# Gates of the recurrent mixer as a seven-product block product, with summed factors kept in DRAM and an output projection over all heads

## The chip, the cores and the metric

One core of a Trainium2 chip runs the whole program. The core has five engines with their own instruction streams: TensorE (PE, matmuls; PEld are its weight loads), VectorE (DVE), ScalarE (ACT), GpSimd (POOL) and SyncE (SP, here only an issuer of DMAs). The metric is the device time of one execution in microseconds; less is better. Times are medians of several runs.

## The reference, cut to what matters

A two-layer encoder over 512 + 256 tokens of width 1024. Each layer is a half-weighted feed-forward, a mixer, and another half-weighted feed-forward, each with its RMS norm and residual. Layer 0's mixer is a bidirectional gated linear recurrence with eight heads of 128, layer 1's is windowed attention. The change is in the recurrent mixer:

```python
def hgrn2_mixer(x, w_in, w_o, g_norm, lb):
    q, i, g, f_fw, f_bw = jnp.split(x @ w_in, 5, axis=-1)
    ...
    o_fwd = gla_chunk_scan(q, k_f, i, logf_f)
    o_bwd = rev(gla_chunk_scan(rev(q), rev(k_b), rev(i), rev(logf_b)))
    o = (o_fwd + o_bwd).astype(F32)
    o = o * lax.rsqrt(jnp.mean(o * o, axis=-1, keepdims=True) + NORM_EPS)
    o = o * g_norm.astype(F32).reshape(H, V)
    o = o.reshape(B, T, H * V).astype(x.dtype) * jax.nn.silu(g)
    return o @ w_o
```

`g` is the gate: 768 tokens by 1024 columns of x times a 1024 by 1024 piece of `w_in`.

## The kernel before, in words

The 768 tokens are 6 blocks of 128, in two halves of three blocks. Float32 matmuls are made of three: each operand is split into a high and a low part, and high x high, high x low and low x high are summed in one PSUM bank (`mm3`, L307 to L311). The lower part of a weight is a VectorE subtraction after a ScalarE cast (L172 and L173 for a piece of 128x1024; L314 and L315 for pieces that lie in other buffers).

The recurrent mixer (`hgrn`) goes through these stages. Chunks of head 0 are projected. The value projection is a block product of 2x2 blocks by seven products instead of eight (`tok_quad`): the token operands are four plain blocks or sums of them (b00, b10, b11 and the sums t1 to t4, named in `FACTOR`), the weight operands are sums of weight blocks made on VectorE (L255), and the products are combined by adds from PSUM. Its matmuls have line L729. Then come eight scans, one a head (`hgrn_scan`). A scan has seven levels; at each, VectorE multiplies packed keys and queries by decay factors (L848, L852), ScalarE copies the packed part (L826), TensorE makes the scores (L796), and VectorE copies them under a mask (L815). After the levels, keys are turned (L868), block states are made (L876, L887) and outputs (L900). `weave` puts a fixed number of pieces of other matmuls between the steps of a scan: the projection chunks of the next heads, and beside head 7 the first half of the gates.

The gates are two plain projections of 512 columns (`proj_tok`, "g0" and "g1"): eight k-tiles of three matmuls for each block. ScalarE takes the Silu from PSUM (L995), VectorE multiplies value, inverse RMS and gate, 128 columns at a time (L1001), TensorE turns the result (L1019), and ScalarE and VectorE write its high and low parts (L1022, L1023). The output projection (`out_proj`) goes twice through both column halves, for heads 0 to 3 and 4 to 7, and adds each to x in a separate addition (L570). x itself lies in DRAM during the mixer and is reloaded by ScalarE's queue.

A scheduler decides the order of the instructions on each engine from the order in which the code issues them and from when buffers come free. What bounds it: 21 arena slots of 6144 bytes a partition ("big"), 8 weight slots of 4096 bytes ("w"), 4 raw weight buffers ("wr"), 8 temporaries ("tA") and 8 PSUM banks ("ps"). Weight loads go out on SP in the order planned by `plan_hgrn`, as far ahead as raw buffers allow; every engine's queue is served in order.

Of the kernel before, what the change touches and what calls it, by code (L numbers as in the profile page):

```python
# [50 lines left out]
class Trunk:  # L51
# [73 lines left out]
    def load_masks(self):  # L125
        raw, self.masks = self.big([P, LEVELS + 1, P]), self.big([P, LEVELS + 1, P], U8)
        self.nc.scalar.dma_start(raw, self.consts[1])
        self.nc.gpsimd.tensor_copy(self.masks, raw)
# [280 lines left out]
    def operand(self, name, k):  # L409
        t = self.ops[(name, k // 2)]  # L410
        return t[:, k % 2, 0, :], t[:, k % 2, 1, :]
# [301 lines left out]
    def tok_quad(self, key, tile):  # L713
        nc = self.nc
        cols = lambda b, c: tile(b)[:, c * 512 : (c + 1) * 512]
        banks = {}
        for name in TOK:
            ws = [self.take((*key, name, kp)) for kp in range(2)]
            chain = {"p2": "p1", "p4": "p5", "p3": "p7"}.get(name, name)
            for i in range(HB):  # L720
# [16 lines left out]
                x11, x12, x21, x22 = cols(i, 0), cols(HB + i, 0), cols(i, 1), cols(HB + i, 1)  # L737
                if name == "p1":
                    nc.scalar.activation(x22, ps, AF.Copy, scale=-1.0)
                elif name == "p2":  # L740
                    nc.scalar.copy(x11, ps)
                elif name == "p4":
                    nc.vector.tensor_add(x21, ps, x22)
                elif name == "p3":
                    nc.vector.tensor_sub(x12, ps, x22)
                elif name == "p5":
                    nc.vector.tensor_sub(x22, x22, ps)
                else:
                    nc.vector.tensor_add(x22, ps, x22)
            for kp in range(2):  # L750
                self.done((*key, name, kp))
            yield name
# [45 lines left out]
    def hgrn_scan(self, hd, v):  # L798
# [63 lines left out]
        kT = self.big([P, 8, P])  # L862
        S = self.big([P, 8, P])
# [37 lines left out]
        for s, (off, n) in enumerate(SEQS):  # L901
            nb = n // P
            sq = self.tmp(n)
            nc.scalar.square(sq, pos[s])
            for b in range(nb):
                nc.scalar.copy(vb(off // P + b), pos[s][:, b * P : (b + 1) * P])
            nc.vector.tensor_reduce(
                self.hss[:, h, off // P : off // P + nb], sq.rearrange("p (b j) -> p b j", b=nb), AX.X, ALU.add
            )

    def plan_hgrn(self, w_in, w_o):
# [6 lines left out]
        rows = w_in[:, D : 2 * D].rearrange("(k m a p) c -> k m p a c", k=2, m=2, p=P)  # L918
        srcs = [[rows[k][m][:, :, c * 512 : (c + 1) * 512] for m in range(2)] for c in range(2) for k in range(2)]
        self.plan_quad(("v",), srcs, None, TOK)  # L920
# [4 lines left out]
        self.plan_tok("g0", w_in, 2 * D)  # L925
        self.plan_tok("g1", w_in, 2 * D + 512)
        self.plan_out("hg_o", w_o)

    def plan_out(self, tag, w_o):
        for half in range(2):  # L930
            for c in range(2):
# [9 lines left out]
    def hgrn(self, lb_row, gn_row, next_row):  # L941
# [19 lines left out]
        for name in self.tok_quad(("v",), vtile):  # L961
            if name == "p6":
# [11 lines left out]
        feed = stream()  # L974
        lead = 4
# [12 lines left out]
        uT = {}  # L988

        def put_g(half):  # L990
            us = {}

            def f(s, b, ps):
                sg = self.tmp(512)
                nc.scalar.activation(sg, ps, AF.Silu)  # L995
                off, n = SEQS[s]
                nb = n // P
                u = self.tmp(512)
                for i in range(4):
                    h = half * 4 + i  # L1000
                    nc.vector.scalar_tensor_tensor(  # L1001
                        u[:, i * P : (i + 1) * P],
                        vs[off // P + b][:, h * P : (h + 1) * P],
                        rs[:, h, off // P + b : off // P + b + 1],
                        sg[:, i * P : (i + 1) * P],
                        ALU.mult,
                        ALU.mult,
                    )
                us[(s, b)] = u
                if b < nb - 1:  # L1010
                    return
                def rest():
                    for i in range(4):
                        h = half * 4 + i
                        if s == 0:
                            uT[h] = self.big([P, 2, T], F32R)
                        pt = self.ps(n)
                        for bb in range(nb):
                            nc.tensor.transpose(pt[:, bb * P : (bb + 1) * P], us[(s, bb)][:, i * P : (i + 1) * P], self.ident)  # L1019
# [409 lines left out]
```

## Time and profile before

| what | value |
|---|---|
| median of 3 runs | 2788.37 us (2788.32 to 2788.64) |
| profiled execution | 2788.47 us |
| its span, first to last instruction | 2786.7 us |
| TensorE busy | 2762.9 us, 99% |
| weight loads of TensorE | 2569.4 us, 92% |
| VectorE busy | 2191.5 us, 79% |
| ScalarE busy | 1343.8 us, 48% |
| GpSimd busy | 376.8 us, 14% |
| granted TensorE clock | 0.999 |
| DMA, mean over the span | 106 GB/s |

Of the span, the recurrent mixer takes about 490 to 1035 us: the value projection 542 to 599, the scans 599 to 935, the second half of the gates and the output projection after that. A group's row in the profile gives line, engine, operation, output <- input with shapes and count, then busy time in us and mean length in ns, then the time that the engine was idle just before, and who ended it. In the chain of waits a row is start, length, engine, line and count; a row of stretches gives the busy time and count of each engine in order, the granted clock, the DMA share and the rate.

### The profile page before, as it was taken

How to read it: one execution, taken by the hardware profiler on the slowest of the kernel's cores; microseconds unless marked ns; L12 is line 12 of the kernel's file. 1: busy time of each engine (PE TensorE's matmuls, PEld its weight loads, DVE VectorE, ACT ScalarE, POOL GpSimd, SP SyncE). 2: the span in 40 equal slices, each digit the busy share in tenths (PEclk: the TensorE clock that was granted, in tenths of full speed). 3: DMA queues.
4: the chain of work that ended last, by engine and by line, in shares of the span. 5: the costliest groups of instructions: out<-in, count | busy, mean ns of one | idle time of the engine just before them, and what ended most of it. 6: DMA issues, size and time to landing. Idle time of an engine off the chain costs nothing.

```text
span 2786.7 us, 40646 instructions
## 1 busy us (share of the span) xinstructions
PE 2762.9 (99%) x15189; PEld 2569.4 (92%) x15189; DVE 2191.5 (79%) x3803; ACT 1343.8 (48%) x2479; POOL 376.8 (14%) x409
## 2 busy tenths in 40 slices
PE   8999999999999999999999999999999999999998
PEld 8999999989999889999999999999988889999998
DVE  8788788777887658878878887887848878778877
ACT  7344444634444435444444643444458855444443
POOL 2111111100000001211111121111002311211110
PEclk9999999999999999999999999999999999999999
DMA  6554554421111223555444365545422122655543
GB/s 176 125 131 114 123 144 128 145 69 39 39 39 31 81 81 81 144 134 124 121 114 121 84 144 127 131 114 122 129 72 76 40 66 74 148 133 129 117 114 107
DMA packets 331750, 294.53 MB, mean 106 GB/s; under 512 B 11848, under 2 KB 258080, under 8 KB 331552
## 3 DMA queue, kind: packets, MB, share of 16 engines
q1 hardware_dynamic: 294560, 213.42, 25.7%
q0 software_dynamic: 32688, 65.03, 13.9%
q10 hardware_dynamic: 4304, 13.49, 1.3%
q8 instruction: 119, 1.95, 0.3%
q14 instruction: 79, 0.65, 0.1%
HBM read 217.44 MB, written 9.44 MB: 81 GB/s over the span
## 4 chain that ended last, share of the span: by engine, by line
PE 96%; DVE 2%; ACT 1%; DMA 0%; issue 0%; DVEq 0%; ACTq 0%
PE ps L486 42%; PE ps L550 21%; PE ps L310 8%; PE ps L309 8%; PE ps L311 8%; PE ps L796 3%; PE ps L729 2%; PE ps L900 1%; PE ps L1291 1%; PE ps L876 1%; PE ps L380 1%; PE ps L1303 0%; PE ps L1253 0%; PE ps L1254 0%; PE ps L1304 0%; PE ps L1054 0%
## 5 line engine op out<-in xcount | busy, mean ns | idle before, releaser
L486 PE MATMUL ps<-big,w 128*128 128x384 f32 x6720 | 1169.3, 334 | 0.0
L486 PEld LDWEIGHTS ps<-big,w 128*128 128x128 f32 x6720 | 1165.9, 188 | 1.7 <-ACT tA L503 0.2
L205 ACT CAST w<-wr 128x512 fp32r<-128x512 f32 x600 | 416.9, 707 | 680.1 <-PE ps L486 277.7
L550 PE MATMUL ps<-w,big 128*128 128x512 f32 x2520 | 575.3, 389 | 0.0
L550 PEld LDWEIGHTS ps<-w,big 128*128 128x128 f32 x2520 | 472.8, 188 | 97.4
L206 DVE TENSOR_TENSOR w<-wr,w 128x512 fp32r<-128x512 f32 (+1 forms) x520 | 429.3, 830 | 159.4 <-ACT w L205 138.9
L572 DVE SCALAR_TENSOR_TENSOR x<-ps,x 128x512 f32<-128x512 f32 x468 | 302.5, 687 | 10.0 <-PE ps L311 9.9
L144 POOL DMA_DIRECT2D s<-wr x122 | 106.7, 877 | 1483.3 <-DMA wr<-in_ffn_w_dram 650.0
L309 PE MATMUL ps<-big,w 128*128 128x384 f32 x640 | 219.5, 345 | 1.1 <-ACT w L172 1.0
L310 PE MATMUL ps<-big,w 128*128 128x384 f32 x640 | 215.6, 337 | 0.6 <-DVE big L315 0.5
L311 PE MATMUL ps<-big,w 128*128 128x384 f32 x640 | 214.6, 335 | 0.0
L309 PE MATMUL ps<-w,big 128*128 128x512 f32 x528 | 210.9, 399 | 0.3 <-DVE big L1314 0.2
L311 PE MATMUL ps<-w,big 128*128 128x512 f32 x528 | 207.0, 392 | 0.5 <-DVE big L395 0.5
L310 PE MATMUL ps<-w,big 128*128 128x512 f32 x528 | 206.4, 391 | 0.0
L314 ACT CAST big<-tA 128x384 fp32r<-128x384 f32 x296 | 148.0, 513 | 113.8 <-DVE tA L518 36.2
L315 DVE TENSOR_TENSOR big<-tA,big 128x384 fp32r<-128x384 f32 x296 | 165.5, 570 | 6.7 <-ACT big L314 4.5
L206 POOL TENSOR_TENSOR w<-wr,w 128x512 fp32r<-128x512 f32 x80 | 133.3, 1666 | 185.8 <-ACT w L205 185.6
L144 POOL DMA_DIRECT2D wr<-wr x101 | 88.6, 877 | 422.0 <-DVE w L206 159.4
L172 ACT CAST w<-wr 128x1024 fp32r<-128x1024 f32 x84 | 88.2, 1052 | 107.3 <-PE ps L310 78.0
L173 DVE TENSOR_TENSOR w<-wr,w 128x1024 fp32r<-128x1024 f32 x84 | 102.1, 1223 | 41.7 <-ACT w L172 36.7
L212 DVE TENSOR_TENSOR wr<-wr,wr 128x512 f32<-128x512 f32 (+1 forms) x120 | 127.4, 1061 | 6.0 <-issue 5.7
L310 PEld LDWEIGHTS ps<-big,w 128*128 128x128 f32 x640 | 120.5, 188 | 1.9 <-DVE big L315 1.7
(198 smaller groups left out, 3390.8 us busy)
## 6 DMA issues: line engine op xcount, KB each, us to landing
wr<-in_ffn_w_dram SPq DMA_DIRECT2D x264, 512.0 KB, 3.9
s<-wr POOLq DMA_DIRECT2D x122, 256.0 KB, 4.8
s<-in_ffn_w_dram SPq DMA_DIRECT2D x120, 256.0 KB, 3.2
wr<-wr POOLq DMA_DIRECT2D x80, 256.0 KB, 3.9
wr<-in_hg_w_in_dram SPq DMA_DIRECT2D x36, 512.0 KB, 3.7
wr<-wr POOLq DMA_DIRECT2D x21, 512.0 KB, 4.6
spill<-x ACTq DMA_DIRECT2D x12, 512.0 KB, 4.0
x<-spill ACTq DMA_DIRECT2D x12, 512.0 KB, 3.2
```

The costliest lines, as they stand in the source:

```text
L144: self.nc.gpsimd.dma_start(out, src, accum_op=ALU.add)
L205: nc.scalar.copy(h, src)
L206: (eng or nc.vector).tensor_sub(l, src, h.bitcast(F32))
L212: add = {"second": lambda: nc.vector.tensor_add(a11, a11, a21), "fourth": lambda: nc.vector.tensor_add(a12, a12, a11)}
L309: nc.tensor.matmul(out, a[0], b[0], start=first, stop=False)
L310: nc.tensor.matmul(out, a[0], b[1], start=False, stop=False)
L311: nc.tensor.matmul(out, a[1], b[0], start=False, stop=last)
L314: self.nc.scalar.copy(hi, src)
L315: self.nc.vector.tensor_sub(lo, src, hi.bitcast(F32))
L486: self.nc.tensor.matmul(ps, a[x], b[y], start=first and k == 0 and i == 0, stop=k == 3 and i == 2, skip_group_check=True,)
L550: nc.tensor.matmul(ps, a[x], w[y], start=name == chain and kp == 0 and q == 0, stop=kp == 1 and q == 2, skip_group_check=True,)
L572: self.nc.vector.scalar_tensor_tensor(x, ps, c, x, ALU.mult, ALU.add)
```

## The change

It does five things. The gates become a second call of `tok_quad`, over all 1024 columns, with seven products in the order p1, p2, p7, p6, p5, p4, p3; it stops after each half of a bank so that it can be woven into head 7's scan like the projection chunks. The four summed token factors t1 to t4 are written to DRAM at the start of the value projection (eight GpSimd DMAs of 128x1536 numbers, 768 KB each) and read back on SP for the gates, each one product ahead of its use. The gating is taken apart: head outputs are scaled by their inverse RMS in place on ScalarE (`scaled`, 48 of 128x128), the Silu is taken of finished quarters, and 12 VectorE multiplies of 128x512 gate them (`gated`); turning goes by half of the tokens and half of the heads (`turned`). The output projection sums all eight heads in one PSUM bank (`out_cols`), so that x gets 12 additions instead of 24. Smaller ones: x is reloaded in two pieces, masks lie in another buffer, and squares lie in enlarged arena tiles.

```diff
+    def spill_factors(self):
+        self.kept = {}
+        for name in ("t3", "t2", "t1", "t4"):
+            for kp in range(2):
+                t = self.kept[(name, kp)] = self.dp.tile([P, 4 * H], F32, name=self.name("kept"))
+                self.nc.gpsimd.dma_start(t, self.ops[(name, kp)].bitcast(F32).rearrange("p a b c -> p (a b c)"))
+
+    def reload_factor(self, name):
+        for kp in range(2):
+            t = self.ops[(name, kp)] = self.big([P, 2, 2, H], F32R)
+            self.nc.sync.dma_start(t.bitcast(F32).rearrange("p a b c -> p (a b c)"), self.kept[(name, kp)])
...
-    def reload_x(self):
-        for b in range(NBLK):
+    def reload_x(self, blocks=range(NBLK)):
+        for b in blocks:
...
-            for kp in range(2):
-                self.done((*key, name, kp))
-            yield name
+                    if k == 1:
+                        if used and i:
+                            self.done(used.pop(0))
+                        yield name, i, 0
+                evac(name, i, ps)
+                if i == HB - 1:
+                    used += [(*key, name, kp) for kp in range(2)]
+                if i == HB - 1 or (used and not i):
+                    self.done(used.pop(0))
+                yield name, i, 1
+        for k in used:
+            self.done(k)
...
-        kT = self.big([P, 8, P])
-        S = self.big([P, 8, P])
+        kT = self.big([P, 12, P])
+        S = self.big([P, 12, P])
+        squares = kT[:, 8:, :], S[:, 8:10, :]
...
+        quad(("g",), 2 * D)
+        self.plan_out("hg_o", w_o, True)
...
+        self.spill_factors()
+        for at in self.tok_quad(("v",), evac_v):
+            if at == ("p6", HB - 1, 1):
...
+        def evac_g(name, i, ps):
+            if name == "p1":
+                if i == 0:
+                    gq["x22"] = wide()
+                nc.scalar.activation(gq["x22"][:, i], ps, AF.Copy, scale=-1.0)
+                return
+            if name == "p2":
+                if i == 0:
+                    gq["x11"] = wide()
+                nc.scalar.activation(gq["x11"][:, i], ps, AF.Silu)
+                return
+            x22 = gq["x22"][:, i]
+            if name == "p5":
+                nc.vector.tensor_sub(x22, x22, ps)
+                if i == 0:
+                    gq["s22"] = wide()
+                nc.scalar.activation(gq["s22"][:, i], x22, AF.Silu)
+                gated(1, 1, i)
+            elif name in ("p4", "p3"):
+                q = "x21" if name == "p4" else "x12"
+                if i == 0:
+                    gq[q] = wide()
+                t = gq[q][:, i]
+                if name == "p4":
+                    nc.vector.tensor_add(t, ps, x22)
+                else:
+                    nc.vector.tensor_sub(t, ps, x22)
+                nc.scalar.activation(t, t, AF.Silu)
+                gated(int(name == "p3"), int(name == "p4"), i)
+            else:
+                nc.vector.tensor_add(x22, ps, x22)
+
+        def gated(half, part, i):
+            b = half * HB + i
+            sg = gq["s22" if half and part else f"x{part + 1}{half + 1}"][:, i]
+            u = vs[b][:, part * 512 : (part + 1) * 512]
+            nc.vector.tensor_mul(u, u, sg)
...
+        def scaled(part, blocks):
+            for b in blocks:
+                for h in range(4 * part, 4 * part + 4):
+                    u = vs[b][:, h * P : (h + 1) * P]
+                    nc.scalar.activation(u, u, AF.Copy, scale=rs[:, h, b : b + 1])
...
+        def turned(half, part):
+            for h in range(4 * part, 4 * part + 4):
+                if half == 0:
+                    uT[h] = self.big([P, 2, T], F32R)
+                pt = self.ps(H)
+                for i in range(HB):
+                    src = vs[half * HB + i][:, h * P : (h + 1) * P]
+                    nc.tensor.transpose(pt[:, i * P : (i + 1) * P], src, self.ident)
+                gn = self.cols[:, gn_row + h : gn_row + h + 1]
+                hi, lo = (uT[h][:, i, half * H : (half + 1) * H] for i in range(2))
+                nc.scalar.activation(hi, pt, AF.Copy, scale=gn)
+                nc.vector.scalar_tensor_tensor(lo, pt, gn, hi.bitcast(F32), ALU.mult, ALU.subtract)
...
+        def gate():
+            need = {"p1": "t3", "p2": "t2", "p7": "t1", "p6": "t4"}
+            for at in self.tok_quad(("g",), evac_g):
+                if at[1:] == (HB - 1, 1) and at[0] in need:
+                    self.reload_factor(need[at[0]])
+                yield at
+
+        feed = itertools.chain(stream(), gate())
         for h in range(HEADS - 1):
-            pieces = 18 - (2 if h == 0 else 0) - (lead if h == HEADS - 2 else 0)
-            self.weave(scan(heads[h]), feed, pieces)
-        self.drain(feed)
-        rs = self.cp.tile([P, HEADS, NBLK], F32, name="hrs")
-
-        def rstds(half):
-            r = rs[:, half * 4 : half * 4 + 4, :]
-            nc.scalar.activation(r, self.hss[:, half * 4 : half * 4 + 4, :], AF.Sqrt, bias=self.eps, scale=1.0 / P)
-            nc.vector.reciprocal(r, r)
-
+            self.weave(scan(heads[h]), feed, 16 if h == 0 else 18)
...
-        g0 = self.proj_tok("g0", put_g(0))
-        for _ in range(lead):
-            next(g0)
-        self.weave(scan(heads[-1]), g0, 24 - lead)
-        self.drain(g0)
+        scaled(0, range(NBLK))
+        self.weave(scan(heads[-1]), feed, 20)
         rstds(1)
-        self.drain(self.proj_tok("g1", put_g(1)))
-        self.reload_x()
-        self.drain(self.out_proj("hg_o", 0, uT, None))
-        self.drain(self.out_proj("hg_o", 1, uT, next_row))
+        rest = [*range(HB, NBLK), *range(HB)]
+        for i in range(HB):
+            gated(0, 0, i)
+        for at in feed:
+            if rest:
+                scaled(1, rest[:1])
+                del rest[0]
+            if at == ("p5", 1, 0):
+                turned(0, 0)
+            elif at == ("p3", 1, 0):
+                turned(0, 1)
+                self.reload_x(range(HB))
+        wo = self.out_cols("hg_o", uT, next_row)
+        for _ in range(2):
+            next(wo)
+        turned(1, 1)
+        for _ in range(2):
+            next(wo)
+        turned(1, 0)
+        self.reload_x(range(HB, NBLK))
+        self.drain(wo)
...
+    def out_cols(self, tag, act, next_row):
+        for c in range(2):
+            for group in ((0,), (1,), (2,), (3, 4, 5)):
+                banks = {}
+                for half in range(2):
+                    for b in group:
+                        if not half:
+                            banks[b] = self.ps()
+                        sl = slice(b * P, (b + 1) * P)
+                        for i in range(4):
+                            key = (tag, half, c, i // 2)
+                            wh, wl = self.take(key)
+                            t = act[half * 4 + i]
+                            w = wh[:, i % 2, :], wl[:, i % 2, :]
+                            self.mm3(banks[b], (t[:, 0, sl], t[:, 1, sl]), w, half + i == 0, half * i == 3)
+                            if i % 2 and b == NBLK - 1:
+                                self.done(key)
+                        if half:
+                            self.add_x(self.x[b][:, c * 512 : (c + 1) * 512], banks[b], 1.0)
+                            if c:
+                                self.after_block(b, next_row)
+                                if b >= 4:
+                                    self.run_later()
+                        yield
```

The order on the engines shows it at three places. The first is TensorE where head 7's scan turns its keys (`868`/`877` with `ident_r`) and makes block states from them (`876`/`885`); a row is line, operation, output <- inputs and shape. Before:

```order
L310 MATMUL ps_1163_8244<-w_1084_7649,big_701_4785 128x512
L311 MATMUL ps_1163_8244<-w_1083_7648,big_701_4785 128x512
L868 MATMUL ps_1172_8271<-ident_r_84,big_1120_7922 128x128 x4
L868 MATMUL ps_1173_8277<-ident_r_84,big_1120_7922 128x128 x4
L309 MATMUL ps_1163_8244<-w_1097_7767,big_707_4825 128x512
L310 MATMUL ps_1163_8244<-w_1098_7768,big_707_4825 128x512
L311 MATMUL ps_1163_8244<-w_1097_7767,big_707_4825 128x512
L876 MATMUL ps_1174_8283<-x_734_5060,big_1170_8269 128x128
L876 MATMUL ps_1174_8283<-x_737_5076,big_1170_8269 128x128
L876 MATMUL ps_1174_8283<-x_740_5092,big_1170_8269 128x128
```

Now:

```order
L741 MATMUL ps_1168_8290<-w_1152_8184,big_1147_8150 128x512
L741 MATMUL ps_1168_8290<-w_1151_8183,big_1147_8150 128x512
L877 MATMUL ps_1171_8306<-ident_r_84,big_1113_7893 128x128 x4
L877 MATMUL ps_1172_8312<-ident_r_84,big_1113_7893 128x128 x4
L885 MATMUL ps_1173_8318<-x_742_5076,big_1169_8304 128x128
L885 MATMUL ps_1173_8318<-x_745_5092,big_1169_8304 128x128
L885 MATMUL ps_1173_8318<-x_748_5108,big_1169_8304 128x128
L885 MATMUL ps_1173_8318<-x_746_5093,big_1169_8304 128x128
L885 MATMUL ps_1174_8323<-x_745_5092,big_1169_8304 128x128
L885 MATMUL ps_1174_8323<-x_748_5108,big_1169_8304 128x128
```

The three gate matmuls (L309 to L311) that stood between the turning and the states are gone: the states now follow the turning at once, and the matmuls of the seven products (L741, of a factor `big` and weight parts `w`) stand before it. The second is VectorE in the middle of head 7's scan, where `big_1120`/`big_1113` is the query operand, `big_1124`/`big_1125` the score matrix, and L823 and L815 are the masked copies. Before:

```order
L852 TENSOR_TENSOR big_1120_7922<-big_1120_7922,big_1125_7966 128x48x8 x2
L1001 SCALAR_TENSOR_TENSOR tA_1140_8083<-x_740_5092,hrs_7930,tA_1139_8081 128x128 x4
L815 COPY_PREDICATED big_1124_7965<-big_765_5264,ps_1141_8089 128x512
L815 COPY_PREDICATED big_1124_7965<-big_765_5264,ps_1142_8090 128x256
L848 TENSOR_TENSOR big_1119_7921<-big_1119_7921,big_1125_7966 128x2x48x8
L854 TENSOR_TENSOR big_1125_7966<-big_1125_7966 128x2x48
L852 TENSOR_TENSOR big_1120_7922<-big_1120_7922,big_1125_7966 128x24x16 x2
```

Now:

```order
L860 TENSOR_TENSOR big_1113_7893<-big_1113_7893,big_1126_8015 128x48x8 x2
L1050 TENSOR_TENSOR x_748_5108<-x_748_5108,big_1139_8094 128x512
L823 COPY_PREDICATED big_1125_8014<-masks_771_5274,ps_1148_8153 128x512
L316 TENSOR_TENSOR w_1145_8145<-wr_1044_7393,w_1144_8144 128x1024
L823 COPY_PREDICATED big_1125_8014<-masks_771_5274,ps_1149_8154 128x256
L856 TENSOR_TENSOR big_1112_7892<-big_1112_7892,big_1126_8015 128x2x48x8
L1044 TENSOR_TENSOR big_1115_7914<-ps_1150_8167,big_1115_7914 128x512
L862 TENSOR_TENSOR big_1126_8015<-big_1126_8015 128x2x48
L256 TENSOR_TENSOR tA_1045_7395<-tA_1045_7395,tA_1051_7407 128x512
L256 TENSOR_TENSOR tA_1046_7396<-tA_1046_7396,tA_1052_7408 128x512
L823 COPY_PREDICATED big_1125_8014<-masks_771_5274,ps_1153_8190 128x512
L316 TENSOR_TENSOR w_1152_8184<-tA_1045_7395,w_1151_8183 128x512
```

Between the parts of a level there stand now lower parts of weights (L316), weight sums (L256), gatings (L1050) and product sums (L1044), where the gating by 128 columns (L1001) stood. The third is SP, after the last weight load of the gates (`wr_1053`); `kept` are the factors in DRAM, `s3` and `in_ffn_w1` belong to the next feed-forward, `in_hg_w_o` to the output projection:

```order
L232 DMA wr_1053_7411<-in_hg_w_in_dram 128x2x512
L440 DMA big_1135_8063<-kept_733_5047 128x1536
L440 DMA big_1136_8065<-kept_734_5049 128x1536
L192 DMA s3_1276_9048<-in_ffn_w1_dram 128x4x128
L192 DMA s3_1294_9141<-in_ffn_w1_dram 128x4x128
L440 DMA big_1146_8148<-kept_735_5051 128x1536
L440 DMA big_1147_8150<-kept_736_5053 128x1536
L440 DMA big_1161_8251<-kept_737_5055 128x1536
L440 DMA big_1162_8253<-kept_738_5057 128x1536
L158 DMA wr_1201_8525<-in_hg_w_o_dram 128x2x512
L440 DMA big_1178_8354<-kept_739_5059 128x1536
L440 DMA big_1179_8356<-kept_740_5061 128x1536
```

Before, the rows after the gates' weights are those of the output projection alone:

```order
L157 DMA wr_1099_7771<-in_hg_w_in_dram 128x2x512
L157 DMA wr_1114_7891<-in_hg_w_in_dram 128x2x512
L157 DMA wr_1166_8255<-in_hg_w_o_dram 128x2x512
L157 DMA wr_1169_8267<-in_hg_w_o_dram 128x2x512
L157 DMA wr_1178_8311<-in_hg_w_o_dram 128x2x512
L157 DMA wr_1181_8323<-in_hg_w_o_dram 128x2x512
```

Eight reloads have come between them, and two loads for the feed-forward stand between the first and the second factor.

More of the change, by code (lines that the diff above doesn't have):

```diff
@@ L907, in hgrn_scan @@
             nc.vector.tensor_reduce(
[L908 removed]
+                self.hss[:, h, off // P : off // P + nb], sq, AX.X, ALU.add
             )
@@ L924, in plan_hgrn, with plan_out @@
                     chunk(h, c)
[L925 to L931, printed above, removed]
+        quad(("g",), 2 * D)
+        self.plan_out("hg_o", w_o, True)
+    def plan_out(self, tag, w_o, by_cols=False):
+        for one in range(2):
+            for two in range(2):
+                half, c = (two, one) if by_cols else (one, two)
                 for i in range(2):
```

100 lines of the change are left out of this document (36 added, 64 removed).

## The prediction

> **What bounds the kernel now.** I read the engine totals of the page first, then the chain that ended last, then a table of stretches over the mixer.
>
> ```profile
> PE 2762.9 (99%) x15189; PEld 2569.4 (92%) x15189; DVE 2191.5 (79%) x3803; ACT 1343.8 (48%) x2479; POOL 376.8 (14%) x409
> PE 96%; DVE 2%; ACT 1%; DMA 0%; issue 0%; DVEq 0%; ACTq 0%
> core 0: us, PE busy (x) PEld busy (x) DVE busy (x) ACT busy (x) POOL busy (x), PEclk, DMA share, GB/s
> 542.00:600.00 58.00, 58.00 (x261) 48.15 (x261) 38.05 (x51) 24.07 (x34) 1.97 (x1) 1.00 0.25 73
> 848.00:890.00 42.00, 41.52 (x283) 39.86 (x282) 32.72 (x59) 19.13 (x39) 0.00 (x0) 1.00 0.13 38
> 890.00:935.00 45.00, 45.00 (x277) 39.76 (x276) 36.25 (x75) 17.73 (x27) 0.00 (x0) 1.00 0.08 24
> 935.00:980.00 45.00, 45.00 (x223) 37.86 (x222) 21.45 (x50) 17.84 (x33) 0.00 (x0) 1.00 0.41 139
> ```
>
> The first two rows say that TensorE has work in 99% of the span and makes up 96% of the chain. The four stretches are the value projection (542 to 600), the scan of head 6 (848 to 890), the scan of head 7 with the first gate half (890 to 935), and the second gate half (935 to 980). TensorE is full in each, at a granted clock of 1.00, but VectorE stands at 36.25 of 45 us beside the last scan. So a matmul taken out of this part is time taken out, unless VectorE no longer delivers in time.
>
> **The change part by part.** *Matmuls.* The gates were 6 blocks x 2 halves x 8 k-tiles x 3 split terms = 288 matmuls of 128x512. Seven products take 7 x 3 blocks x 4 k-tiles x 3 terms = 252. That is 36 fewer; the output projection and the 48 transposes keep their matmuls. The time of one is read where nothing else is in the way:
>
> ```profile
> 542.15 57.16 PE ps L729 x252
> 81.13 28.60 PE ps L550 x126
> L729 PE MATMUL ps<-w,big 128*128 128x512 f32 x252 | 57.3, 389 | 0.0
> ```
>
> In the chain, 252 such matmuls take 57.16 us and 126 of the feed-forward take 28.60: 0.227 us each, both times. The 389 ns of the grouped row is the modelled length of an overlapping record and is not used. 36 x 0.227 = 8.17 us go. The Trainium skill, "TensorE: Matmul & The Clock Gate", section "Back-to-back issue gap", gives about 131 ns per matmul of 512 columns in a real kernel's stream, and 216 ns for an isolated gap; by these, called estimates, the saving would be 36 x 0.131 = 4.7 us or 36 x 0.216 = 7.8 us. The trace disagrees with the first: its stream runs at 0.227, and the measurement decides.
>
> *VectorE beside the last scan.* This is where I expect part of it back. The scan has seven levels; each needs a packed multiply, two multiplies and two masked copies from VectorE before TensorE can make the next scores. These rows price them, and what is put between them:
>
> ```profile
> L848 DVE TENSOR_TENSOR big<-big,big 128x768 f32<-128x768 f32 x56 | 53.0, 946 | 2.6 <-ACT big L829 2.6
> L852 DVE TENSOR_TENSOR big<-big,big 128x384 f32<-128x384 f32 x112 | 58.4, 555 | 11.5 <-ACT big L826 8.0 <-DVE big L854 0.5
> L815 DVE COPY_PREDICATED big<-big,ps 128x512 f32<-128x512 uint8 x56 | 41.3, 737 | 19.1 <-PE ps L796 19.1
> L815 DVE COPY_PREDICATED big<-big,ps 128x256 f32<-128x256 uint8 x56 | 24.4, 435 | 0.0
> L1001 DVE SCALAR_TENSOR_TENSOR tA<-x,hrs,tA 128x128 f32<-128x128 f32 x48 | 13.9, 348 | 20.2 <-ACT tA L995 20.2
> L1023 DVE SCALAR_TENSOR_TENSOR big<-ps,cols,big 128x512 fp32r<-128x512 f32 x8 | 5.4, 742 | 0.0
> L173 DVE TENSOR_TENSOR w<-wr,w 128x1024 fp32r<-128x1024 f32 x44 | 53.6, 1223 | 24.2 <-ACT w L172 22.4 <-PE ps L486 1.6
> L315 DVE TENSOR_TENSOR w<-tA,w 128x512 fp32r<-128x512 f32 x12 | 7.7, 687 | 0.1
> L570 DVE TENSOR_TENSOR x<-ps,x 128x512 f32<-128x512 f32 x24 | 16.6, 690 | 26.3 <-PE ps L311 26.3
> ```
>
> A level is 0.946 + 2 x 0.555 + 0.737 + 0.435 = 3.2 us. Between head 7's first masked copy and its state updates, VectorE's order in the kernel before has 16 gating products of 128x128 (16 x 0.348 = 5.6), four lower parts of turned tiles (4 x 0.742 = 3.0) and two lower parts of weights (2 x 1.223 = 2.4): 11.0 us. In the changed order it has eighteen instructions of 128x512 (eight lower parts, five product sums, three gatings, two weight sums, 18 x 0.69 = 12.4) and three of 1024 (3 x 1.22 = 3.7): 16.1 us. That is 5.1 us more, and 36.25 + 5.1 = 41.4 us of a 45 us stretch, 92% instead of 81%. VectorE is still not full, so the 5.1 are not lost as such; what is lost is what comes in front of a level. How much that costs, the kernel before shows once, in its chain:
>
> ```profile
> 866.50 0.70 issue
> 867.20 1.05 ACT w L172
> 868.28 1.23 DVE w L173
> 869.51 0.47 DVE big L852
> 869.97 0.97 DVE big L815 x2
> 870.95 0.84 DVE big L848
> 871.79 0.47 DVE big L852
> 872.37 0.84 ACT big L826
> 873.25 1.60 PE L796 MATMUL ps<-big,big 128*128 128x128 f32 x12 [0.48 <-ACT big L826]
> ```
>
> A weight's lower part (1.23 us) stands ahead of the level's work, the packed copy on ScalarE comes 1.2 us late, and TensorE, which had projection matmuls to fill most of it, waits 0.48 us. In the changed order such a piece stands in front of a level's multiply or masked copy at levels 3 to 7, and in front of head 6's state updates there is a block of multiplies of head 7. Following the seven levels with the durations above and the matmuls that stand between, I get five such waits of 0.35 to 0.9 us, and a sixth of 0.4 where the eight transposes of head 7 are followed at once by the matmuls that read their copy, without filler. Together about 3 us, against 1.2 us of gaps that the kernel before has in the same place: +2 us. The bounds of this term are 0 (all filled by matmuls) and 5.1 us (all of the added VectorE time exposed) plus one whole level, 3.2.
>
> *Factors to DRAM and back.* Eight transfers of 768 KB each way. The nearest rows are of 512 KB:
>
> ```profile
> x<-spill ACTq DMA_DIRECT2D x12, 512.0 KB, 3.2
> wr<-wr POOLq DMA_DIRECT2D x21, 512.0 KB, 4.6
> wr<-in_hg_w_o_dram SPq DMA_DIRECT2D x8, 512.0 KB, 5.4
> ```
>
> 1.5 x 3.2 = 4.8 us for one coming back, 1.5 x 4.6 = 6.9 us for one going out. The Trainium skill, "DMA: Bandwidth & Descriptors", section "Anatomy of one DMA — SWDGE (gpsimd) path", has 2.0 us + bytes / 436e3, by which one of 768 KB would be an estimate of 3.8 us. A pair back is 4.8 to 9.6 us. It is issued a product ahead: one product of 36 matmuls is 8.2 us alone, and over twice that where scan matmuls are woven in. The first factor out must have left before its slots are reused, after the third value product, 3 x 8.2 = 24.5 us on, and the DMA share there is 0.25; the mask conversion queued behind the eight spills on POOL is wanted only after the 57 us of that projection. The third and fourth reload stand behind loads for the next feed-forward and the output projection on SP; those wait for weight buffers that are released a product earlier. Cost taken: 0; bounds: 0, and 4 x 9.6 us less one product, below.
>
> *The rest at nothing.* Scaling the heads is 48 ScalarE instructions of 128x128; a copy of that size:
>
> ```profile
> L906 ACT COPY x<-ps 128x128 f32<-128x128 f32 x48 | 10.1, 302 | 0.0
> ```
>
> 48 x 0.302 = 14.5 us, spread over both scans and the gate's second part, where ScalarE has 17.73 and 17.84 of 45 us; without that cover the last 24 would be 7.2 us. Twelve fewer additions to x (12 x 0.69 = 8.3 us of VectorE) lie in the output projection, beside matmuls; they free nothing that TensorE waits for. The next feed-forward starts in the same order as before.
>
> Sum: the profiled execution took 2788.47 us (span 2786.7 and 1.8 around it), 0.1 above the median. 2788.47 - 8.17 + 2 = 2782.3 us.
>
> **The rivals.** *No new waits:* the filler covers every level, as it does in all scans before (TensorE busy 45.00 of 45 beside 36.25 of VectorE). 2788.4 - 8.2 = 2780.2. Against it: VectorE's load rises to 92% there.
>
> *VectorE becomes the bound of the last scan:* the whole added 5.1 us shows on TensorE: 2788.4 - 8.2 + 5.1 = 2785.3, and with a whole level of 3.2 exposed as well at the start of a product 2788.5, so from no gain to half of it. For it: the 92% and a chain from VectorE over ScalarE to TensorE at each level; against it: only two of the products stand fully in the scan's shadow, and three blocks are interleaved.
>
> *Slower: reloads come late.* SP issues in order. If a load ahead of a factor waits for a buffer that only the running product releases, the factor is issued when it is wanted, and TensorE waits for a pair. Four pairs fully exposed are 4 x 9.6 = 38.4 us, less the 8.2: 2818. It decides from 8.2 + 5.6 = 13.8 us of exposed reload, two late pairs with most of their time; one late pair (9.6) gives 2789.8. For it: two of the four pairs are queued behind other loads, and output weights took 5.4 us to land where a reload of x took 3.2. Against it: in 848 to 935 the DMA is busy 0.08 to 0.13 of the time.
>
> *The change does not do what it says:* excluded, since the order of TensorE holds 36 fewer matmuls of this shape. The skill's 131 ns would leave 2788.4 - 4.7 + 2 = 2785.7; the 0.227 of 252 matmuls in a row excludes it too, under 1 in 100.
>
> **How the numbers follow.** A measurement of this kernel tells 0.2%, 5.6 us, from no change, so faster ends at 2782.8. Forecast 2782.3: 0.47, with a range of its own from 2780.8 to 2784 (waits of 0.6 to 3.8 us), of which 0.37 lie under 2782.8 and 0.10 over. No new waits 0.13. VectorE the bound 0.27, all of it within 0.2%. Late reloads 0.13, of which I put 0.03 at one late pair, within 0.2%, and 0.10 beyond. Faster 0.37 + 0.13 = 0.50, same 0.10 + 0.27 + 0.03 = 0.40, slower 0.10. The range goes from 2779.7 (no waits, less the spread of 0.3 and a little of the kernel before's own gaps) to 2788.6 (VectorE the bound with a level exposed); it leaves out the 0.13 of late reloads.
>
> **What would show it.** The gate products should stand at 0.227 us a matmul where no scan is woven in (p5 to p3), VectorE near 41 of 45 us beside head 7's scan, and gaps of 0.3 to 0.9 us ahead of the scores of levels 4 to 7 with ScalarE's packed copy as the releaser. No wait of TensorE should end on a DMA. If TensorE shows under 0.5 us of gaps there, the second rival holds; if single gaps exceed 1.5 us, VectorE is the bound; if a product's first matmul waits for a reload, the slower one holds. A gain under 4 us with no such gaps would mean that the price of a matmul is wrong.

## The result, and the profile after

The changed kernel takes 2783.76 us (median of 19 runs, 2783.16 to 2784.56) against 2788.39 (19 runs): 4.6 us or 0.17% less, ratio 0.9983 with a 95% interval of 0.9977 to 0.9990. The forecast was 2782.3 us, 6.1 less. The measured time lies in the range; the gain is clear of noise, since the interval leaves out 1, but it is smaller than the 0.2% from which the prediction counts a kernel as faster.

The page and the chain of the changed kernel, with the same rows as before the prediction:

```profile
PE 2755.8 (99%) x15153; PEld 2560.7 (92%) x15153; DVE 2209.6 (79%) x3790; ACT 1365.2 (49%) x2544; POOL 385.3 (14%) x424
PE 96%; DVE 2%; ACT 1%; DMA 0%; issue 0%; DVEq 0%; ACTq 0%; SPq 0%
```

TensorE has 36 instructions fewer, and still makes the time. What the whole span tells only with the feed-forwards' noise on top, two rows of the chain tell exactly: the start of the value projection and the start of the next feed-forward's long stream (start, length, engine, line, count). First the changed kernel, then the end row of the kernel before, whose start row, 542.15, stands in the prediction:

```profile
541.83 57.16 PE ps L741 x252
1071.89 29.12 PE ps L499 x168
```

```profile
1077.11 29.12 PE ps L486 x168
```

From the one start to the other there were 534.96 us and are now 530.06: the mixer is 4.90 us shorter. In a second profile of the changed kernel it was 530.08, 0.02 us away, while its runs spread over 1.4 us. All experiments below are read by this difference, called the mixer's time.

The stretches beside the last two scans and after them, in the changed kernel (busy time and count of PE, PEld, DVE, ACT, POOL, then clock, DMA share, GB/s):

```profile
848.00:890.00 42.00, 41.62 (x279) 39.95 (x278) 33.44 (x60) 18.05 (x33) 0.00 (x0) 1.00 0.08 22
890.00:935.00 45.00, 43.66 (x263) 37.67 (x262) 39.19 (x70) 20.89 (x38) 0.00 (x0) 1.00 0.41 144
935.00:980.00 45.00, 45.00 (x227) 37.21 (x226) 32.85 (x51) 30.97 (x67) 0.00 (x0) 1.00 0.39 123
```

TensorE was full between 890 and 935 us and now has 1.34 us of nothing; VectorE rose from 36.25 to 39.19 us there, not to the 41.4 of the forecast. TensorE's waits in the order of time, with the idle time before each and what ended it:

```profile
888.64 0.49 PE L909 MATMUL ps<-big,big 128*128 128x128 f32 x2 [0.38 <-DVE big L896]
911.12 1.58 PE L804 MATMUL ps<-big,big 128*128 128x128 f32 x12 [0.61 <-DVE big L856]
918.44 1.60 PE L804 MATMUL ps<-big,big 128*128 128x128 f32 x12 [0.29 <-ACT big L834]
923.01 1.60 PE L804 MATMUL ps<-big,big 128*128 128x128 f32 x12 [0.19 <-ACT big L834]
928.47 2.05 PE L885 MATMUL ps<-x,big 128*128 128x128 f32 x16 [0.24 <-ACT big L878]
```

A matmul's record lasts 0.39 us where the next starts after 0.227, so a wait costs about 0.16 us more than the idle time in brackets. With it the five gaps cost 0.54, 0.77, 0.45, 0.35 and 0.40 us, 2.5 in all; the second matmul after each starts another 0.1 late, which makes 3.0. The first stands ahead of head 6's state updates, the next three ahead of the scores of the last three of head 7's seven levels, the fifth ahead of its block states.

### The profile page after: what moved, and what is told of

The parts are those of the page before. It is cut to its first block, busy times and chain, and to the rows that moved or that the text cites. A ratio compares the mean times of both kernels' runs of the same rounds, so it can differ in the third digit from the quotient of the medians.

```text
span 2781.6 us, 40707 instructions
## 1 busy us (share of the span) xinstructions
PE 2755.8 (99%) x15153; PEld 2560.7 (92%) x15153; DVE 2209.6 (79%) x3790; ACT 1365.2 (49%) x2544; POOL 385.3 (14%) x424
## 4 chain that ended last, share of the span: by engine, by line
PE 96%; DVE 2%; ACT 1%; DMA 0%; issue 0%; DVEq 0%; ACTq 0%; SPq 0%
PE ps L499 42%; PE ps L563 21%; PE ps L311 7%; PE ps L310 7%; PE ps L312 7%; PE ps L741 4%; PE ps L804 3%; PE ps L909 1%; PE ps L1385 1%; PE ps L381 1%; PE ps L885 1%; PE ps L1397 0%; PE ps L1347 0%; PE ps L1348 0%; PE ps L1398 0%; PE ps L1123 0%
## 5 line engine op out<-in xcount | busy, mean ns | idle before, releaser
L563 PE MATMUL ps<-w,big 128*128 128x512 f32 x2520 | 575.4, 389 | 0.0
L207 DVE TENSOR_TENSOR w<-wr,w 128x512 fp32r<-128x512 f32 (+1 forms) x520 | 438.7, 847 | 147.9 <-ACT w L206 130.5
L311 PE MATMUL ps<-big,w 128*128 128x384 f32 x640 | 215.5, 337 | 0.9 <-DVE big L316 0.9
L310 PE MATMUL ps<-w,big 128*128 128x512 f32 x432 | 172.1, 399 | 0.3 <-DVE big L1408 0.2
L316 DVE TENSOR_TENSOR big<-tA,big 128x384 fp32r<-128x384 f32 x296 | 166.5, 573 | 6.7 <-ACT big L315 4.5
L312 PE MATMUL ps<-w,big 128*128 128x512 f32 x432 | 169.7, 393 | 0.6 <-DVE big L396 0.5
L311 PE MATMUL ps<-w,big 128*128 128x512 f32 x432 | 168.8, 391 | 0.0
L174 DVE TENSOR_TENSOR w<-wr,w 128x1024 fp32r<-128x1024 f32 x76 | 92.5, 1222 | 47.0 <-ACT w L173 41.7
L311 PEld LDWEIGHTS ps<-big,w 128*128 128x128 f32 x640 | 120.4, 188 | 2.4 <-DVE big L316 2.3
L173 ACT CAST w<-wr 128x1024 fp32r<-128x1024 f32 x76 | 79.8, 1052 | 85.8 <-PE ps L311 55.9
```

The lines of the kernel that those rows point to most:

```text
L207: (eng or nc.vector).tensor_sub(l, src, h.bitcast(F32))
L310: nc.tensor.matmul(out, a[0], b[0], start=first, stop=False)
L311: nc.tensor.matmul(out, a[0], b[1], start=False, stop=False)
L312: nc.tensor.matmul(out, a[1], b[0], start=False, stop=last)
L316: self.nc.vector.tensor_sub(lo, src, hi.bitcast(F32))
L563: nc.tensor.matmul(ps, a[x], w[y], start=name == chain and kp == 0 and q == 0, stop=kp == 1 and q == 2, skip_group_check=True,)
```

## The experiments

**Does a matmul cost 0.227 us on the path?** One product done twice:

```diff
+                    terms = ((h, wh), (h, wl), (l, wh))
+                    if key == ("g",) and name == "p4":
+                        terms = terms[:2] * 2 + terms[2:] * 2
+                    last = len(terms) - 1
...
```

> Product p4 of the gates is done twice into the same banks: 36 matmuls of 128x512 more, outside any scan, as many as the change took out (the gates of one quarter are other numbers). If a matmul costs 0.227 us: plus 8.2 us less the waits for p3's weights that they cover (up to 0.5), 2791.4 to 2792.0. If a matmul costs less than that on the path (0.131): plus 4.7, 2788.5.

Measured 2791.38 us, 7.6 above the changed kernel; its two rows of the chain:

```profile
542.43 57.16 PE ps L745 x252
1080.11 29.12 PE ps L499 x168
```

The mixer takes 537.68 us, 7.62 more, since the added matmuls also cover four small gaps ahead of p3's matmuls (0.08, 0.11, 0.22 and 0.11 us by the starts of the matmuls, 0.52 together). 7.62 + 0.52 = 8.14 for 36 matmuls is 0.226 each. The price of the removed work stands as the forecast took it.

**Do the factors cost anything on their way through DRAM?** Neither written nor read; the products p4 to p7 read a plain block:

```diff
-        self.spill_factors()
...
-                if at[1:] == (HB - 1, 1) and at[0] in need:
-                    self.reload_factor(need[at[0]])
...
+                    if key == ("g",) and fac[0] == "t":
+                        fac = "b10"
```

> The summed factors are neither written to DRAM nor read back; the gate products p4 to p7 read the plain block b10 instead, so the gates are other numbers. Eight transfers of 768 KB each way and their slots go. If the trip is hidden, as forecast: time within 0.5 us of 2783.8 and the same gaps. If it costs (the late reloads): 2 us or more below, 2781.8 or less, with fewer gaps in the gate's later products (937 to 979 us).

Measured 2784.01 us; mixer 530.07, and the same waits:

```profile
911.32 1.57 PE L807 MATMUL ps<-big,big 128*128 128x128 f32 x12 [0.62 <-DVE big L859]
918.64 1.60 PE L807 MATMUL ps<-big,big 128*128 128x128 f32 x12 [0.29 <-ACT big L837]
923.20 1.60 PE L807 MATMUL ps<-big,big 128*128 128x128 f32 x12 [0.20 <-ACT big L837]
```

The trip is free to a hundredth of a microsecond, and the rival of the late reloads falls. The transfers are not quicker than feared; in the changed kernel they land after

```profile
kept<-big POOLq DMA_DIRECT2D x8, 768.0 KB, 5.4
big<-kept SPq DMA_DIRECT2D x8, 768.0 KB, 7.5
```

7.5 us back against my 4.8: it is the product in between that covers them.

**Do twelve additions to x matter?** The output projection of the kernel before, in two passes, with the rest of the change (its weight loads and the last turning then go in the order of the two passes):

```diff
-        wo = self.out_cols("hg_o", uT, next_row)
+        wo = self.out_proj("hg_o", 0, uT, None)
...
+        self.drain(self.out_proj("hg_o", 1, uT, next_row))
```

> The changed kernel with the output projection of the kernel before: two passes over head halves, 24 additions to x. If the twelve additions lay beside matmuls: time within 0.6 us of 2783.8, and the same start of the next feed-forward. If the projection over all heads is worth something, up to 12 x 0.69 = 8.3 us above; if the single bank per block delays the next feed-forward's start (gaps of 0.45 and 0.40 us there against 0.34 and 0.10 before), about 0.4 us below.

Measured 2783.37 us, mixer 529.73 us. The projection over all heads is not worth anything and costs 0.33 us, at the start of the next feed-forward, where a gap of 0.40 us is 0.10 again.

**Is it VectorE's load?** As much VectorE work as the change brought, once more:

```diff
                 nc.vector.tensor_add(x22, ps, x22)
+                nc.vector.tensor_max(x22, x22, x22)
...
             nc.vector.tensor_mul(u, u, sg)
+            if not half and not part:
+                nc.vector.tensor_max(u, u, u)
```

> Each sum of the products p7 and p6 and each of the three gatings beside head 7's scan is followed by one more VectorE instruction of the same size that leaves its data as they are (nine of 128x512, about eight of them beside the scan): 8 x 0.69 = 5.5 us more, as much again as the change added. VectorE's queue as the cause: gaps between 893 and 937 us grow from 2.6 to 5 to 8 us and the time to 2786.5 to 2789. Matmuls hide it: gaps stay under 3.5 us, time under 2785.

Measured 2784.93 us, mixer 531.21, 1.15 more. The waits and the load beside the scan:

```profile
911.61 1.58 PE L804 MATMUL ps<-big,big 128*128 128x128 f32 x12 [0.48 <-DVE big L856]
918.97 1.60 PE L804 MATMUL ps<-big,big 128*128 128x128 f32 x12 [0.33 <-ACT big L834]
924.00 1.60 PE L804 MATMUL ps<-big,big 128*128 128x128 f32 x12 [0.67 <-ACT big L834]
893.00:937.00 44.00, 42.28 (x250) 36.27 (x250) 42.51 (x77) 20.03 (x34) 0.00 (x0) 1.00 0.37 132
```

VectorE stands at 42.5 of 44 us, and the scan's gaps grow by 0.4 us, from the 2.6 of the text above to 3.0; the rest of the 1.15 comes after the scan. So the second case expected there held, and the 5 to 8 us of gaps of the first did not come. Where the nine instructions went tells why. Five stand behind the last level (from 928.79 us on). One, at 904.88, takes the place of a gating, which the scheduler moves behind the scan. Only three, at 912.14, 919.29 and 923.02, stand among the levels, and none of them ahead of the first of the three waits there. More load on VectorE is not by itself what costs, but this run does not tell what one more instruction ahead of that first wait would cost.

**Is it what stands in front of one level?** The chain of the changed kernel ahead of its largest wait:

```profile
904.99 0.35 DVE big L862
905.34 1.13 DVE wr L256
906.47 0.94 DVE big L860 x2
907.41 0.60 DVE x L1050
908.01 0.66 DVE big L823
908.67 1.10 DVE w L316
909.77 0.36 DVE big L823
910.13 0.85 DVE big L856
910.98 0.14 issue
911.12 0.91 PE ps L804 x6
```

The level's own rows are L862, L860, L823 and L856; a weight sum (L256, 1.13), a gating (L1050, 0.60) and a lower part of a weight (L316, 1.10) stand between them, 2.8 us. Two kernels take one kind of these away. The first holds the three gatings, which all stand ahead of this wait (from 901.83 to 907.33 us), back to the end of the scan:

```diff
-            nc.vector.tensor_reduce(
+            self.last_sum = nc.vector.tensor_reduce(
...
-        for i in range(HB):
-            gated(0, 0, i)
+        with self.tc.issue_after(self.last_sum):
+            for i in range(HB):
+                gated(0, 0, i)
```

> The three gatings of 128x512 that VectorE does beside head 7's scan are held back until that scan's last VectorE instruction; nothing else changes. If a level waits for what stands in front of it (in the changed kernel one gating, a weight sum of 1.22 and a lower part of 1.22 stand in front of the level whose scores wait 0.78 us), that gap falls by about 0.6 us to 0.2 and the time by 0.5 to 0.8 us, to 2783.1. If the total VectorE time counts, 3 x 0.69 = 2.1 of 39.2 us less gives the same. If neither does (doubling the added VectorE work moved the scan's gaps by 0.4 us only), the gaps between 893 and 937 us stay at 2.6 us.

Measured 2782.04 us, mixer 528.36, 1.70 less. Its waits between 885 and 940 us, and a stretch of the levels, 897 to 924 us, in the changed kernel and in this one:

```profile
888.84 0.49 PE L909 MATMUL ps<-big,big 128*128 128x128 f32 x2 [0.39 <-DVE big L896]
926.85 2.05 PE L885 MATMUL ps<-x,big 128*128 128x128 f32 x16 [0.24 <-ACT big L878]
897.00:924.00 27.00, 25.90 (x145) 21.75 (x144) 26.36 (x46) 12.33 (x18) 0.00 (x0) 1.00 0.52 172
897.00:924.00 27.00, 27.00 (x156) 23.42 (x156) 26.30 (x46) 12.60 (x18) 0.00 (x0) 1.00 0.43 147
```

All three waits at the levels are gone, not the first alone, though nothing was taken away between the first and the last. The three gaps were one delay: a level that is late hands its lateness to the next, and TensorE waits each time its filler runs out. The two rows of stretches also show what the 87% of the longer stretch hides: in the middle of the scan VectorE was full in both kernels, 26.36 and 26.30 of 27 us, and TensorE waited in the one and not in the other. On a full queue it is the order that decides, what is done before a level's own instructions and what after them. The second makes the weight sums by adding transfers instead of VectorE additions:

```diff
-            if name in sums:
+            if name in sums and key == ("v",):
...
+            ahead = {"p2": "p6", "p5": "p3"}.get(name)
+            if ahead and key == ("g",):
+                for t, u in zip(sums[ahead][0][kp], sums[ahead][1][kp]):
+                    self.into(t, u)
```

> The four weight sums of the gates (p6 and p3) are made by adding transfers issued from GpSimd's queue right after p2's and p5's weights are staged, in place of VectorE additions. VectorE loses 1.22 + 2 x 0.69 = 2.6 us beside the scan, and as much in the gate's later products. Theory (what stands in front of a level): the 0.78 us gap goes, and the late lower parts in the tail come earlier; gaps fall by 1 to 1.5 us in all, time 2782.5. Rival: the transfers land too late, or their issue on GpSimd slows VectorE as the GpSimd sums did; then a product's first matmul waits for ScalarE's cast, and the time rises by 1 us or more.

Measured 2781.60 us, mixer 527.76, 2.30 less. It takes away the same three gaps and most of those in the later products, where a weight load waited for the cast and the lower part of p3's weights; these two rows of the changed kernel's weight loads are not in it any more:

```profile
954.23 0.30 PEld L741 LDWEIGHTS ps<-w,big 128*128 128x128 f32 x2 [0.34 <-ACT w L315]
955.49 0.53 PEld L741 LDWEIGHTS ps<-w,big 128*128 128x128 f32 x3 [0.28 <-DVE w L316]
```

**The sums and gatings on GpSimd.**

```diff
+                eng = nc.gpsimd if key == ("g",) else nc.vector
...
-                    self.tc.keep_in_program_order(nc.vector.tensor_add(t, t, u))
+                    self.tc.keep_in_program_order(eng.tensor_add(t, t, u))
...
-            nc.vector.tensor_mul(u, u, sg)
+            (nc.vector if half or part else nc.gpsimd).tensor_mul(u, u, sg)
```

> The four weight sums of the gate products and the three gatings that fall beside head 7's scan go from VectorE to GpSimd; all else as in the changed kernel. If the waits beside that scan come from instructions queued in front of a level on VectorE, VectorE there loses about 3 x 0.69 + 1.22 + 2 x 0.69 = 4.7 us, TensorE's gaps between 893 and 937 us fall from 2.6 us to 1.5 or less, and the time goes from 2783.8 to about 2782.7. If the waits come from the factors' way through DRAM or from the weights' loads, the gaps stay at 2.6 us. If a GpSimd sum (1.7 us for 512 columns in the feed-forward) is late for the weight it makes, a product's first matmul waits up to 2 us and the time rises.

Measured 2788.12 us, mixer 534.23: 4.17 more, nearly the whole gain. GpSimd is busy with the sums from 911.41 to 917.85 us, and VectorE beside it, in rows of the timeline:

```profile
911.41 2.80 POOL L257 TENSOR_TENSOR wr<-wr,wr 128x1024 f32<-128x1024 f32 x1
914.17 3.68 POOL L257 TENSOR_TENSOR tA<-tA,tA 128x512 f32<-128x512 f32 x2
911.92 1.05 DVE L824 COPY_PREDICATED big<-masks,ps 128x512 f32<-128x512 uint8 x2
912.87 2.16 DVE L857 TENSOR_TENSOR big<-big,big 128x768 f32<-128x768 f32 x1
914.95 1.75 DVE L317 TENSOR_TENSOR w<-tA,w 128x512 fp32r<-128x512 f32 x1
920.09 0.95 DVE L857 TENSOR_TENSOR big<-big,big 128x768 f32<-128x768 f32 x1
915.17 1.58 PE L805 MATMUL ps<-big,big 128*128 128x128 f32 x12 [2.82 <-DVE big L857]
```

The same multiply takes 2.16 us beside GpSimd and 0.95 without, a lower part 1.75 instead of 0.69, and TensorE waits 2.82 us. A sum at 837.26 us does the same to an earlier head's scan: its multiply takes 2.42 us, and TensorE waits 1.42 us at 842.46. With it the loss is nearly accounted for, by the starts of the matmuls: 3.1 us more beside head 7's scan, 1.5 more in the earlier one, 0.6 less in the gate's later products. Taking work off VectorE made VectorE slower. The Trainium skill, "SBUF — State Buffer", section "SBUF: two separate sides", says that VectorE and GpSimd share a port pair that one of them holds for a whole instruction, and that VectorE instructions with two SBUF inputs need it too when the GpSimd instruction reads SBUF. These rows agree: the multiply ends 0.82 us after the first GpSimd sum does (915.03 against 914.21 us), about its own 0.95, and the masked copy beside it, whose scores come from PSUM (L824), keeps its 1.05 us for two.

**Two changes of the order alone.** Weights released half a product earlier:

```diff
+                        if i == HB - 1 and key == ("g",):
+                            self.done((*key, name, 0))
                         yield name, i, 0
...
+                    if key == ("g",):
+                        self.done((*key, name, 1))
```

> The weights of a gate product are released half a product earlier (the first k pair after the last matmul that reads it, the second at the product's end), so that the next weights are cast earlier. If the small gaps in p5 to p3 (0.7 us between 937 and 979 us, ScalarE's cast and VectorE's lower part as releasers) come from late staging, they go and the time falls by 0.5 to 0.7 us, to 2783.1; beside the scan the earlier lower parts stand in front of other levels, so the gaps there move and their sum stays within 1 us of 2.6. If they come from the factors' reloads, nothing changes.

and one more hand-over in head 7's scan, ahead of the block states:

```diff
+        if h == HEADS - 1:
+            yield
         pds = []
...
-        self.weave(scan(heads[-1]), feed, 20)
+            self.weave(scan(heads[-1]), feed, 20, LEVELS + 2)
```

> Head 7's scan hands over to the gate products once more, between the turning of the keys and the block states, and its 20 pieces are spread over nine steps instead of eight. If the 0.40 us ahead of the states comes from the missing filler, it goes to about 0.1 as in the other heads, and the time falls by 0.3 us; the other gaps beside the scan shift, since each step gets fewer pieces, and stay between 1.5 and 3 us.

They measured 2785.11 and 2785.05 us, mixer 530.38 and 531.86. Each has one large wait in the levels; first the earlier release with the chain ahead of it, then the further hand-over:

```profile
906.28 1.02 DVE big L865 x2
907.30 0.60 DVE x L1055
907.90 1.14 DVE w L316
909.04 1.20 DVE tA L256 x2
910.24 0.65 DVE big L828
910.89 1.17 DVE w L316 x2
912.06 0.35 DVE big L828
912.41 0.86 DVE big L861
913.41 1.58 PE L809 MATMUL ps<-big,big 128*128 128x128 f32 x12 [2.41 <-DVE big L861]
```

```profile
920.62 1.89 PE L804 MATMUL ps<-big,big 128*128 128x128 f32 x12 [2.35 <-ACT big L834]
922.00:926.00 4.00, 4.00 (x14) 3.22 (x13) 2.98 (x6) 0.00 (x0) 0.00 (x0) 0.60 0.73 223
```

Both did what they were made for: the gaps ahead of p3 are gone in the one, the wait ahead of the states in the other. Both pay at a level: with the earlier release 0.60 + 1.14 + 1.20 + 1.17 = 4.1 us of other work stand inside one, where it was 2.8, and one wait of 2.41 us replaces three that were shorter. This is the same cause in the other direction, by a change of the order with no work added. Of the 1.35 us of the earlier release only 0.32 lie in the mixer. The rest lies outside it and does not come in every execution: five of the eleven runs took 2784.1 to 2784.4 us, the others 2785.1 to 2786.3; what makes it stays open. In the further hand-over the last row, a stretch of 4 us right after the wait, shows a granted clock of 0.60: matmuls there start 0.43 us apart instead of 0.227, which makes about 1.5 of its 1.80 us. Waits as long in two other kernels (2.41 and 2.82 us) are followed by no such stretch, so it isn't the wait alone; what it was stays open, and so does whether every execution has it (the runs spread from 2783.66 to 2786.27 us).

**The three gains together:** sums by transfers, gatings held back, output projection in two passes.

> The weight sums by adding transfers, the three gatings held back, and the output projection in two passes, together. If the effects add: about 1.2 us (sums) + 0.6 (gatings) + 0.4 (two passes) below the changed kernel, 2781.6; the least that it can be is 2780.5, the changed kernel without any gap that the kernel before does not have. If the chain of the levels sets the scan whatever stands beside it: 2783.4, as with the two passes alone.

Measured 2781.22 us, ratio to the kernel before 0.9974 (0.9964 to 0.9985); on the same chip the changed kernel once more:

> The changed kernel once more, beside the others on the same chip: 2783.8, gaps as before.

had 2783.86, 0.9984 (0.9975 to 0.9992). The mixer takes 527.53 us, 7.43 less than before the change, from these two rows:

```profile
541.77 57.16 PE ps L745 x252
1069.30 29.12 PE ps L503 x168
```

The gains do not add (2.30 + 1.70 + 0.33), since two of them remove the same delay, and gatings that come later hold up the turning at 944 us by 0.2.

## Why the prediction was right or wrong

The terms below are counted by the starts of TensorE's matmuls: what lies between two starts beyond the usual distance, which is 0.227 us for 512 columns.

*The matmuls:* right; an experiment had 0.226 us for each of 36, the sum 0.227.

*The waits beside the last scan:* right in place, but that the net came near 2 us is luck. Six gaps of 0.35 to 0.9, 3 us in all, less 1.2 that the kernel before has there, were forecast. There are five of 0.35 to 0.77, 3.0 us with what follows each, and those at the levels are ahead of the last three, where four or five were forecast; the largest is ended by VectorE's multiply and not by ScalarE's copy. The kernel before does have 1.2 us there by this count, but in small delays of about 0.1 us each, and the changed kernel still has 1.0 us of such. So from 885 to 937 us it has 4.0 against 1.2: 2.7 more where I took 2. Head 6's scan, from 848 to 885, gives 1.0 back, which was not forecast: the wait of 0.48 us quoted in the prediction is gone.

*The reason given*, the added VectorE time on the way to 92%, was only half of it. Over 45 us the load reached 87%, but in the middle of the scan VectorE was full, and it was as full in the kernel without waits at the levels. What costs is what the order puts inside one level, three instructions, and that level's lateness passed on.

*The step that failed* is "the rest at nothing". In the later products, p5 to p3, TensorE loses 1.1 us more than the kernel before in the same stretch, 0.5 of it ahead of p3's matmuls, where I wrote that no scan is woven in and the stream should stand at 0.227: p3's weights are late there. And "the next feed-forward starts in the same order as before" was true and no argument: in the same order it has 0.4 us more of gaps, and two passes of the output projection take most of it back (0.33); how the single bank per block delays the start was not followed further. With 0.1 in the scans of the other heads, -8.2 + 2.7 - 1.0 + 1.1 + 0.4 + 0.1 = -4.9, the mixer's measured difference.

*The rivals:* no new waits is wrong by the 3.3 us that came. VectorE as the bound is wrong as named: VectorE was full for 27 us, yet the order alone decided whether TensorE waited. Its time, 2785.3, was as far off, 1.5 us, as mine, on the other side. Late reloads are excluded by the trip left out. The 131 ns of the Trainium skill ("TensorE: Matmul & The Clock Gate", section "Back-to-back issue gap") for a matmul in a stream are not seen in this case's traces: doubling a product cost 226 ns for each.

## What to carry to other kernels

Where one engine feeds another through a chain of levels, count what the order puts between the instructions of a level, and not only the engine's load. Here three instructions inside one level cost 1.6 us in three places, while nine more elsewhere, three of them among the levels, cost 0.4 us beside the scan. An average can hide a full queue: 87% over 45 us was 98% over 27. When work must leave VectorE, giving it to transfers or to a later time paid here (2.3 and 1.7 us); giving it to GpSimd slowed VectorE itself and cost 4.2. And measure between two landmarks of the chain: in two profiles of the changed kernel they agreed to 0.02 us, where its runs spread by 1.4.

## What the runs showed that I had not expected

VectorE instructions on two SBUF operands took 2.3 to 2.5 times as long while a GpSimd sum ran (0.95 to 2.16 us, 0.69 to 1.75). A factor of 768 KB lands after 7.5 us although x's 512 KB take 3.2, and it makes no difference.
